# Layer 0 input stage: x before the adaLN loads, filter work mixed in by time, query latents stored to DRAM

## The chip, the cores and the metric

The kernel runs on one core of one Trainium2 chip. A core has five engines, each with its own instruction stream: TensorE (PE in the profile, with PEld for its weight loads), VectorE (DVE), ScalarE (ACT), GpSimd (POOL) and SyncE (SP). Here SP issues nearly all transfers and POOL a few; 16 DMA engines carry them. The metric is the time of one launch in microseconds on the device.

## The reference

A two-layer trunk over 1024 latent tokens and 256 context tokens of width 1024, in float32. Layer 0 is multi-head latent attention, layer 1 a Hyena long convolution. What matters here:

```python
shift, scale, gate = split((silu_c @ ada_w[i] + ada_b[i]), 3)       # adaLN, both layers
a  = modulate(rmsnorm(x, norm_g[0]), shift, scale)                  # latents
ac = modulate(rmsnorm(ctx, norm_g[0]), shift_c, scale_c)            # context
cq, ckv, k_rope, gate = split(t @ mla_w_in, splits)                 # t = a, then ac
q  = rmsnorm(cq, q_norm_g) @ w_uq;  kv = rmsnorm(ckv, kv_norm_g) @ w_ukv
...                                                                 # attention, output, residual
h = sin-MLP(features) @ hy_filt_w_out * decay                       # layer 1's filters
spec = rfft(k_circ(h))                                              # independent of x
```

## The kernel before

Tensors lie with channels on the 128 partitions. A matrix product is made of three float32r matmuls on high and low parts (`mm3`, L119 to L121): an operand is split by ScalarE (`hi`, L96) and VectorE (`lo`, L97). The program is written as Python generators that take turns. A scheduler then orders the instructions of each engine when the program is built, mostly in the order of writing, and fills in later ones where an engine would be free.

The stage in question is `layer0_in` (L440), about the first 440 us. It does three kinds of work side by side.

- **adaLN** (`ada`, L145): for k = 0 to 7 it loads a row block of the adaLN matrix and adds four packed matmuls (L128) to one PSUM bank `ad`; then it copies, transposes (L165) and adds the bias into `adac` and the gain `gs` (L171, L176). Layer 0's shift and scale take 32 pages of 128x512 (`pg<-in_adaw`). The rest (layer 1, and the gates) takes 32 tiles of 128x1024 (`aw`, two buffers).
- **Projections**: x is loaded in two halves of 512 tokens, normed (`rms`, L361; `spread`, L395) and modulated (`modulate`, L403) to `ax`, and `project` (L410) makes 14 column blocks: gates 0 to 7 (`gates`, stored to `gate_d`), the latents of key and value and the rotary key (`latent_kv`, stored to `ckv_d`, `kr_d`), and the query latents (`latent_q`). `context` does the same for the context tokens. Weights come through `wr` (two buffers) and are split to `w`.
- **Filters** (`filters`, L284): an MLP, then eight groups g. A group is eight steps j (load `dec`, four matmuls to `ph`, product `kk` at L321, sum and difference `kp`, `km`), a ring of vector sums (`ring`, L217), and eight blocks i, each split (`bh`, `bl`), multiplied with the matrices `fm` (`forward`, L267, PSUM `u`), scaled to `ko` and stored to `kd`. `rp`'s tiles have two buffers, `dec` too.

What sets the order: half 0 of x and its norm, then the 32 adaLN pages with a filter step after each k, and half 1 of x after k = 7. From then on one step of `work()` is taken for every two filter steps (`n * 120 < (step + 1) * 60`). When the filters are done their SBUF is given to the attention's tiles (`attention_loads`, L626): POOL loads `ckv`, `krh` and `krl`; the query latents come last and are split into SBUF tiles `cq` beside gates 6 and 7. SP is in order: a transfer that waits holds all behind it.

Of the kernel before, what the change touches and what calls it, by code (L numbers as in the profile page):

```python
# [11 lines left out]
F32 = mybir.dt.float32  # L12
# [43 lines left out]
class Net:  # L56
# [60 lines left out]
    def mm3(self, out, w, x, start, stop):  # L117
        mm = self.nc.tensor.matmul
        mm(out, lhsT=w[0], rhs=x[0], start=start, stop=False)  # L119
        mm(out, lhsT=w[0], rhs=x[1], start=False, stop=False)  # L120
        mm(out, lhsT=w[1], rhs=x[0], start=False, stop=stop)  # L121
# [23 lines left out]
    def ada(self, parts, page, bank, width):  # L145
# [138 lines left out]
    def filters(self, psum, pt_h, pt_u, side):  # L284
# [7 lines left out]
        for c in (slice(13, 19), slice(19, 25), slice(0, 7), slice(7, 13)):  # L292
            for i in range(2):
                nc.gpsimd.tensor_copy(out=fm[i][0:1, c.start, 0:1], in_=last[0:1, 0:1])
                nc.gpsimd.dma_start(out=fm[i][:, c], in_=a["fm"][i][:, c])
# [12 lines left out]
        for g in range(KD):  # L308
# [3 lines left out]
            for j in range(8):  # L312
                dec = rp.tile([P, 2, 1, P], F32, tag="dec", name="dec", bufs=2)
# [18 lines left out]
                yield  # L332
# [4 lines left out]
            def emit(i, b):  # L337
                u = self.forward(two, ubank, fm, i, b)
# [70 lines left out]

    def project(self, srcs, bank):  # L410
# [29 lines left out]
    def layer0_in(self):  # L440
# [12 lines left out]
        self.ckv_d = [self.dram.tile([KKV, P, NK], F32, name=f"ckv_d{r}") for r in range(2)]  # L453
        self.kr_d = [self.dram.tile([65, NK], F32, name=f"kr_d{r}") for r in range(2)]
        self.silu_c()
        self.feed([a["w1"][m] for m in (0, 1, 2, 8, 9, 10, 3, 4, 8, 9, 10, 5, 11, 12, 13, 6, 7)])
# [15 lines left out]
        load_x(0)  # L472
        rx = [self.rms(x[0], 512, bank, page)]
        filt.send(x[0][7])
        for n, _ in enumerate(self.ada([(0, 0, 4)], lambda n: page(), abank, 512)):
            next(filt)
            if n == 7:
                load_x(1)
# [937 lines left out]
```

## Time and profile before

| | us |
|---|---|
| median of 3 runs | 1739.24 (1736.87 to 1746.16) |
| the profiled execution | 1735.72 |
| its span, first to last instruction | 1733.9 |
| first projection matmul of layer 0 | 78.1 |
| last filter transform | 407.3 |
| first attention matmul on the stored latents | 436.6 |

A row of a table of groups reads: line, engine, operation, output<-inputs, shape, count, then busy time, mean ns of one, and idle time of the engine before it with what ended it. A row of the timeline reads: start, length, engine, line, operation, count, and in brackets the idle time before it and what ended that. In a table by stretch each engine has its busy time, with the number of instructions in brackets.

### The profile page before, as it was taken

Reading aid. Unit: us, or ns where it says so; the run is one execution under the profiler, and the core shown is the slowest. Engines: PE = TensorE matmul, PEld = TensorE weight load, DVE = VectorE, ACT = ScalarE, POOL = GpSimd, SP = SyncE. Lnnn points to the kernel's source line nnn. Section 1 sums busy time; section 2 is a strip of 40 time slices with the busy share of each in tenths; the row PEclk is TensorE's granted clock in tenths of the full one; section 3 lists DMA queues with packets and bytes.
Section 4 is the critical chain, followed back from the end, with each engine's and each line's share of the span. In section 5 each row is a group of like instructions: output and inputs, shape, how many; then the busy total and the mean of one; then the engine's idle time right before and its main releaser. Section 6 shows DMA issues by size and latency. Waiting matters only on the chain.

```text
span 1733.9 us, 22766 instructions
## 1 busy us (share of the span) xinstructions
PE 1635.3 (94%) x8096; PEld 1300.2 (75%) x8096; DVE 1442.4 (83%) x2539; ACT 766.1 (44%) x1331; POOL 15.4 (1%) x43
## 2 busy tenths in 40 slices
PE   6799897898999999999999999999999999999995
PEld 2467676686788788788787777888888888887873
DVE  4885978895598899899889466999999999999856
ACT  4533444435455555455556345433433433433313
POOL 1000000000000000000000010000000000000000
PEclk8899998999999999999999999999999999999998
DMA  9777563436101001010013781332332332334555
GB/s 341 255 231 222 182 191 118 147 95 196 37 22 42 25 26 37 25 33 25 19 56 121 233 268 64 101 97 84 100 117 83 104 111 85 102 113 138 175 158 204
DMA packets 139030, 207.19 MB, mean 119 GB/s; under 512 B 13386, under 2 KB 67361, under 8 KB 138788
## 3 DMA queue, kind: packets, MB, share of 16 engines
q1 hardware_dynamic: 135780, 195.05, 35.7%
q0 software_dynamic: 3136, 10.69, 1.9%
q8 instruction: 64, 1.05, 0.2%
q14 instruction: 50, 0.41, 0.1%
HBM read 149.97 MB, written 53.61 MB: 117 GB/s over the span
## 4 chain that ended last, share of the span: by engine, by line
PE 79%; DMA 8%; DVE 8%; ACT 3%; issue 1%; SPq 1%; DVEq 0%; ACTq 0%
PE pj L121 13%; PE pj L119 13%; PE pj L120 12%; PE O L120 2%; PE S L119 2%; PE O L119 2%; PE S L811 2%; DMA kd<-ko 2%; PE O L121 2%; PE apx L747 2%; PE S L810 2%; PE S L121 2%; PE S L120 2%; PE apx L748 2%; DMA aw<-in_adaw 2%; PE fu L119 2%
## 5 line engine op out<-in xcount | busy, mean ns | idle before, releaser
L96 ACT CAST w<-wr 128x512 fp32r<-128x512 f32 (+1 forms) x154 | 93.7, 609 | 259.2 <-PE pj L120 134.3
L119 PE MATMUL pj<-a,w 128*128 128x512 f32 x512 | 203.3, 398 | 1.7 <-ACT a L407 1.6
L121 PE MATMUL pj<-a,w 128*128 128x512 f32 x512 | 203.3, 398 | 0.0
L120 PE MATMUL pj<-a,w 128*128 128x512 f32 x512 | 203.2, 397 | 0.0
L813 ACT ACTIVATE p<-S 128x512 f32<-128x512 f32 x160 | 95.5, 597 | 148.2 <-DVE acc L820 69.5
L97 DVE TENSOR_TENSOR w<-wr,w 128x512 fp32r<-128x512 f32 (+1 forms) x154 | 102.4, 673 | 56.5 <-ACT w L96 56.3
L96 ACT CAST bh<-raw 128x512 fp32r<-128x512 f32 x128 | 77.0, 620 | 88.8 <-DVE raw L1056 71.1
L119 PEld LDWEIGHTS pj<-a,w 128*128 128x128 f32 x512 | 96.5, 189 | 22.0 <-ACT a L407 2.4
L120 PEld LDWEIGHTS pj<-a,w 128*128 128x128 f32 x512 | 96.6, 189 | 19.8 <-DVE a L408 0.2
L121 PEld LDWEIGHTS pj<-a,w 128*128 128x128 f32 x512 | 96.7, 189 | 19.4 <-issue 0.8
L97 DVE TENSOR_TENSOR p<-p 128x512 fp32r<-128x512 f32 x160 | 109.5, 685 | 1.5 <-ACT p L96 1.2
L749 DVE TENSOR_REDUCE cm<-apx 128x1 f32<-128x512 f32 (+1 forms) x192 | 107.3, 592 | 3.8 <-PE apx L748 3.0
L121 PE MATMUL pj<-pg,w 128*128 128x512 f32 (+1 forms) x248 | 98.0, 395 | 9.5 <-DVE w L97 9.5
L820 DVE TENSOR_TENSOR acc<-acc,p 128x512 f32<-128x512 f32 x144 | 98.9, 687 | 7.6 <-ACT p L813 6.7
L96 ACT CAST p<-p 128x512 fp32r<-128x512 f32 x160 | 99.4, 622 | 4.8
L119 PE MATMUL pj<-pg,w 128*128 128x512 f32 (+1 forms) x248 | 96.7, 393 | 2.4 <-ACT pg L407 2.4
L120 PE MATMUL pj<-pg,w 128*128 128x512 f32 (+1 forms) x248 | 98.1, 396 | 0.6 <-DVE pg L408 0.6
L97 DVE TENSOR_TENSOR bl<-raw,bh 128x512 fp32r<-128x512 f32 x128 | 84.9, 688 | 9.1 <-ACT bh L96 8.9
L119 PE MATMUL u<-bh,fm 128*128 128x256 f32 (+1 forms) x200 | 67.8, 340 | 11.6 <-ACT bh L96 9.0
L321 DVE TENSOR_TENSOR kk<-ph,dec 128x512 f32<-128x512 f32 x64 | 42.9, 685 | 35.4 <-DMA dec<-in_dec 28.2
L747 PE MATMUL apx<-kn,qn 128*128 128x512 f32 (+1 forms) x192 | 69.1, 364 | 2.3 <-DVE cm L749 1.9
L748 PE MATMUL apx<-krh,r 128*128 128x512 f32 (+1 forms) x192 | 67.2, 358 | 0.0
(304 smaller groups left out, 4392.4 us busy)
## 6 DMA issues: line engine op xcount, KB each, us to landing
aw<-in_adaw SPq DMA_DIRECT2D x32, 512.0 KB
kd<-ko SPq DMA_DIRECT2D x128, 128.0 KB
wr<-in_hw SPq DMA_DIRECT2D x64, 256.0 KB
kt<-kd SPq DMA_DIRECT2D x56, 256.0 KB
wr<-in_w SPq DMA_DIRECT2D x34, 256.0 KB
dec<-in_dec SPq DMA_DIRECT2D x64, 128.0 KB
pg<-in_adaw SPq DMA_DIRECT2D x32, 256.0 KB
wr<-in_wo SPq DMA_DIRECT2D x32, 256.0 KB
```

The costliest lines, as they stand in the source:

```text
L96: self.nc.scalar.copy(out=hi, in_=raw)
L97: self.nc.vector.tensor_tensor(out=lo, in0=raw, in1=hi, op=ALU.subtract)
L119: mm(out, lhsT=w[0], rhs=x[0], start=start, stop=False)
L120: mm(out, lhsT=w[0], rhs=x[1], start=False, stop=False)
L121: mm(out, lhsT=w[1], rhs=x[0], start=False, stop=stop)
L321: nc.vector.tensor_tensor(out=kk, in0=ps, in1=dec.broadcast_to([P, 2, 2, P]), op=ALU.mult)
L747: mm(b[:, :w], lhsT=qn[0][:, c], rhs=kn[0][:, o : o + w], start=True, stop=False)
L748: mm(b[:, :w], lhsT=r1[:, c], rhs=krh[:, o : o + w], start=False, stop=True)
L749: v.tensor_reduce(out=cm[:, t, i : i + 1], in_=b[:, :w], axis=AX.X, op=ALU.max)
L810: mm(S, lhsT=krh[:, c], rhs=r1, start=False, stop=False)
L813: act.activation(out=p, in_=S, func=AF.Exp, scale=ASCALE)
L820: v.tensor_tensor(out=acc, in0=acc, in1=p, op=ALU.add)
```

## The change

1. Both halves of x are loaded and multiplied by their inverse norm in place (`normalize`) before the adaLN loads. The modulate is then `shifted`: the high part by ScalarE with gain and shift, the same in place by VectorE (TENSOR_SCALAR), and the difference. Context does so inside `context`.
2. During layer 0's adaLN loads, the filters take a step only after every second k. The matrices `fm` are loaded in step j = 4 of group 0 rather than at the start, on POOL, behind a read of the last tile of x.
3. `ada` yields between its loads and its matmuls. For the later parts (`late`) the loads keep their written order, and the matmuls are placed behind the last matmul of a projection or filter (`self.last`). A step is taken at every third work step from the thirteenth on.
4. Filter steps yield a cost (1.5 for a step j, 9.0 to 1.5 for a block, ahead of it), and work steps are taken in proportion to the sum of costs: 61 over the stage. A filter block's matmuls are placed behind `self.last`.
5. `latent_q` runs in the middle, is stored to `cq_d` in DRAM as high and low parts, and POOL reloads it to `cq`. Gates 6 and 7 come after the attention loads.

PE runs the same 7928 matmuls, VectorE 2565 instructions in place of 2541, ScalarE 1331 in place of 1333 (two table loads fewer), POOL six more loads and SP twelve more stores.

```diff
-        self.feed([a["w1"][m] for m in (0, 1, 2, 8, 9, 10, 3, 4, 8, 9, 10, 5, 11, 12, 13, 6, 7)])
+        self.feed([a["w1"][m] for m in (0, 1, 8, 9, 10, 2, 3, 8, 9, 10, 11, 12, 13, 4, 5, 6, 7)])
...
-                    nc.sync.dma_start(out=w, in_=self.a["adaw"][layer, k, :, o : o + wd])
+                    dma = nc.sync.dma_start(out=w, in_=self.a["adaw"][layer, k, :, o : o + wd])
+                    if late:
+                        self.tc.keep_in_program_order(dma)
...
-            self.packed([(ps[32 * q : 32 * q + 32, :], self.sc[:, k, :], w, k == 0, k == KD - 1)
-                         for q, w in enumerate(cols)])
             yield
+            with self.tc.issue_after(self.last.ins) if late else ExitStack():
+                self.packed([(ps[32 * q : 32 * q + 32, :], self.sc[:, k, :], w, k == 0, k == KD - 1)
+                             for q, w in enumerate(cols)])
...
             for j in range(8):
+                if (g, j) == (0, 4):
+                    for c in (slice(13, 19), slice(19, 25), slice(0, 7), slice(7, 13)):
+                        for i in range(2):
+                            nc.gpsimd.tensor_copy(out=fm[i][0:1, c.start, 0:1], in_=last[0:1, 0:1])
+                            nc.gpsimd.dma_start(out=fm[i][:, c], in_=a["fm"][i][:, c])
...
-                yield
+                yield 1.5
...
-                u = self.forward(two, ubank, fm, i, b)
+                with self.tc.issue_after(self.last.ins):
+                    u = self.forward(two, ubank, fm, i, b)
...
+                yield {4: 9.0, 0: 2.1, 1: 2.1, 2: 2.8, 3: 2.1}.get(i, 1.5)
                 emit(i, b)
-                yield
...
+    def shifted(self, x, gs, sh, hi, lo):
+        nc = self.nc
+        nc.scalar.activation(out=hi, in_=x, func=AF.Identity, scale=gs, bias=sh)
+        nc.vector.tensor_scalar(out=x, in0=x, scalar1=gs, scalar2=sh, op0=ALU.mult, op1=ALU.add)
+        nc.vector.tensor_tensor(out=lo, in0=x, in1=hi, op=ALU.subtract)
...
+        for h, xs in enumerate(x):
+            load_x(h)
+            self.normalize(xs, self.rms(xs, 512, bank, page), bank)
+        begun = False
+        for n, _ in enumerate(self.ada([(0, 0, 4)], lambda n: page(), abank, 512, False)):
+            if n % 2:
+                if begun:
+                    next(filt)
+                else:
+                    filt.send(x[1][7])
+                    begun = True
...
+            yield from gates(range(0, 2))
             yield from latent_kv()
+            yield from gates(range(2, 4))
             yield from context()
+            yield from latent_q()
+            yield from gates(range(4, 6))
...
+        n, t, whole = 0, 0.0, 8 * (8 * 1.5 + 22.6) - 6.0
+        for cost in filt:
+            t += cost
+            while n * whole < t * 61:
                 next(todo, None)
                 n += 1
+                if n > 12 and n % 3 == 0:
+                    next(vecs, None)
...
+        for k in range(KQ):
+            for r in range(2):
+                nc.gpsimd.dma_start(out=cq[r][k], in_=self.cq_d[r][k])
```

How the change moves instructions is shown at three places. First SP's queue at the start of the program, where `in_xT` is x, `in_adaw` the adaLN matrix, `dec` the decay table of one filter step, `wr` a projection weight. Before, from the first half of x on:

```order
L466 DMA pg<-in_xT 128x512 x8
L303 DMA fwr<-in_fwout 128x512
L314 DMA dec<-in_dec 128x256
L324 DMA hbias<-in_hbias 1x2x128
L314 DMA dec<-in_dec 128x256
L112 DMA wr<-in_w 128x512 x2
L156 DMA aw<-in_adaw 128x1024 x2
L156 DMA pg<-in_adaw 128x512 x8
L314 DMA dec<-in_dec 128x256
L156 DMA pg<-in_adaw 128x512 x4
```

And in the changed kernel, from the same transfer on:

```order
L486 DMA pg<-in_xT 128x512 x8
L302 DMA fwr<-in_fwout 128x512
L318 DMA dec<-in_dec 128x256
L328 DMA hbias<-in_hbias 1x2x128
L318 DMA dec<-in_dec 128x256
L112 DMA wr<-in_w 128x512 x2
L486 DMA pg<-in_xT 128x512 x8
L318 DMA dec<-in_dec 128x256 x2
L302 DMA fwr<-in_fwout 128x512
L328 DMA hbias<-in_hbias 1x2x128
L156 DMA pg<-in_adaw 128x512 x32
L318 DMA dec<-in_dec 128x256 x2
```

The second half of x has moved ahead of the adaLN pages, which now stand in one piece behind two `dec` loads; the two early `aw` tiles are gone from there.

Second, VectorE where the adaLN result (`adac`, `gs`) arrives. In the changed kernel:

```order
L174 TENSOR_TENSOR adac_89<-ad,cols 128x4x4 x2
L179 SCALAR_TENSOR_TENSOR gs_90<-adac_89,cols 128x8
L332 TENSOR_TENSOR kp_342<-kk 128x256
L179 SCALAR_TENSOR_TENSOR gs_90<-adac_89,cols 128x8
L333 TENSOR_TENSOR km_344<-kk 128x256
L97 TENSOR_TENSOR fw<-fwr,fw 128x512
L97 TENSOR_TENSOR w<-wr,w 128x512
L426 TENSOR_SCALAR pg<-pg,gs_90,adac_89 128x512
L427 TENSOR_TENSOR pg<-pg 128x512
```

Before, at the same place:

```order
L171 TENSOR_TENSOR adac_87<-ad,cols 128x4x4
L176 SCALAR_TENSOR_TENSOR gs_88<-adac_87,cols 128x8
L321 TENSOR_TENSOR kk<-ph,dec 128x512
L388 RECIPROCAL rms<-rms 128x4
L176 SCALAR_TENSOR_TENSOR gs_88<-adac_87,cols 128x8
L328 TENSOR_TENSOR kp_954<-kk 128x256
L389 TENSOR_TENSOR rms<-rms 128x4
L97 TENSOR_TENSOR bl<-blk,bh 128x512
```

There filter group 0's blocks (`bl`) and the norm of the second half stand around it, and the modulate follows some fifteen instructions later; in the changed kernel the modulate follows at once and group 0's ring and blocks come between and after its tiles.

Third, POOL behind the filters. Before:

```order
L641 DMA ckv_3999<-ckv_d_81 128x1280
L641 DMA ckv_4000<-ckv_d_81 128x1280
L646 DMA krh<-kr_d_82 64x1280 x2
L647 DMA krl<-kr_d_83 65x1280
L969 CAST dm_9857<-x_9866 1x1
```

Changed:

```order
L657 DMA krh<-kr_d_84 64x1280 x2
L658 DMA krl<-kr_d_85 65x1280
L662 DMA cq_4332<-cq_d_82 128x1024
L662 DMA cq_4335<-cq_d_83 128x1024
L662 DMA cq_4333<-cq_d_82 128x1024
L662 DMA cq_4336<-cq_d_83 128x1024
L662 DMA cq_4334<-cq_d_82 128x1024
L662 DMA cq_4337<-cq_d_83 128x1024
```

The six reloads of the query latents stand last, behind the loads of the key and value latents.

More of the change, by code (lines that the diff above doesn't have):

```diff
@@ L120, in mm3 @@
         mm(out, lhsT=w[0], rhs=x[1], start=False, stop=False)
-        mm(out, lhsT=w[1], rhs=x[0], start=False, stop=stop)
+        self.last = mm(out, lhsT=w[1], rhs=x[0], start=False, stop=stop)
     def packed(self, mms):
@@ L143, in silu_c, with ada @@
                      for i in range(2)]
-    def ada(self, parts, page, bank, width):
+    def ada(self, parts, page, bank, width, late=True):
         nc = self.nc
@@ L291, in filters @@
         last = yield
[L292 to L295, printed above, removed]
         two = lambda tag, dt=F32: rp.tile([P, 2, CS], dt, tag=tag, name=tag)
@@ L408, in modulate, with normalize @@
         nc.vector.scalar_tensor_tensor(out=lo, in0=x, scalar=sh, in1=hi, op0=ALU.add, op1=ALU.subtract)
+    def normalize(self, xs, r, bank):
+        n = xs[0].shape[-1]
+        R = self.spread(r, n // P, bank)
+        for x in xs:
+            self.nc.vector.tensor_tensor(out=x, in0=x, in1=R[:, :n], op=ALU.mult)
+    def shifted(self, x, gs, sh, hi, lo):
[3 more added lines that the diff above has]
+        nc.vector.tensor_tensor(out=lo, in0=x, in1=hi, op=ALU.subtract)
     def project(self, srcs, bank):
@@ L453, in layer0_in @@
         self.ckv_d = [self.dram.tile([KKV, P, NK], F32, name=f"ckv_d{r}") for r in range(2)]
+        self.cq_d = [self.dram.tile([KQ, P, L], F32, name=f"cq_d{r}") for r in range(2)]
         self.kr_d = [self.dram.tile([65, NK], F32, name=f"kr_d{r}") for r in range(2)]
         self.silu_c()
-        self.feed([a["w1"][m] for m in (0, 1, 2, 8, 9, 10, 3, 4, 8, 9, 10, 5, 11, 12, 13, 6, 7)])
+        self.feed([a["w1"][m] for m in (0, 1, 8, 9, 10, 2, 3, 8, 9, 10, 11, 12, 13, 4, 5, 6, 7)])
         filt = self.filters(ps, "ph", "pu", "right")
@@ L509, in normed @@
             for k, t in enumerate(xs):
-                if sbuf:
-                    self.split(t, dst[0][k][:, sl], dst[1][k][:, sl])
-                else:
-                    hilo_out(t, P, [d[k, :, sl] for d in dst])
+                hilo_out(t, P, [d[k, :, sl] for d in dst])
         def context():
-            R = self.spread(rc, 2, bank)
+            self.normalize(xcs, self.rms(xcs, LC, bank, page), bank)
+            yield
             ac = [[], []]
@@ L571, in latent_q @@
                 yield
-            more = gates(range(6, 8))
             for h, sl in enumerate(halves):
-                for _ in normed([t[h] for t in ts], "qg", self.att[3], sl, True):
-                    next(more, None)
-                    yield
-            yield from more
+                yield from normed([t[h] for t in ts], "qg", self.cq_d, sl)
         def gates(ms):
@@ L588, in work @@
         def work():
[L589 to L592 removed]
+            yield from gates(range(0, 2))
             yield from latent_kv()
[L594 to L596 removed]
+            yield from gates(range(2, 4))
             yield from context()
[L598 to L607 removed]
+            yield from latent_q()
+            yield from gates(range(4, 6))
+        todo = work()
+        vecs = chain(self.ada([(1, 0, 4)], awt, abank, 1024), self.ada([(0, 4, 2), (1, 4, 2)], awt, abank, 1024))
+        n, t, whole = 0, 0.0, 8 * (8 * 1.5 + 22.6) - 6.0
+        for cost in filt:
+            t += cost
+            while n * whole < t * 61:
                 next(todo, None)
                 n += 1
+                if n > 12 and n % 3 == 0:
+                    next(vecs, None)
         for _ in todo:
+            pass
+        for _ in vecs:
             pass
@@ L618, in layer0_in @@
         next(loads)
-        for _ in latent_q():
-            next(loads, None)
         for _ in loads:
+            pass
+        for _ in gates(range(6, 8)):
             pass
```

37 lines of the change are left out of this document (5 added, 32 removed).

## The prediction

> **What bounds the kernel now.** I read the page's first two parts, then a table of busy time by stretch, then the timeline at the stretches' edges.
>
> ```profile
> span 1733.9 us, 22766 instructions
> PE 1635.3 (94%) x8096; PEld 1300.2 (75%) x8096; DVE 1442.4 (83%) x2539; ACT 766.1 (44%) x1331; POOL 15.4 (1%) x43
> PE   6799897898999999999999999999999999999995
> DVE  4885978895598899899889466999999999999856
> DMA  9777563436101001010013781332332332334555
> ```
>
> TensorE is 9 tenths busy nearly everywhere after slice 10 (a slice is 43.3 us). The gaps lie in the first ten slices, which are the layer 0 input stage, and that is the only place the change touches. Behind the first attention keys the built order of the two kernels is the same on every engine. The table below cuts that stage at the ends of the eight filter groups (the last split of a group, `bl`), from 107.5 us on; the two columns to compare are PE busy and DVE busy.
>
> ```profile
> core 0: us, PE busy (x) PEld busy (x) DVE busy (x) ACT busy (x) POOL busy (x), PEclk, DMA share, GB/s
> 0.00:61.00 61.00, 37.25 (x145) 14.01 (x145) 34.77 (x73) 24.00 (x39) 5.76 (x20) 0.80 0.98 339
> 61.00:78.00 17.00, 15.74 (x107) 11.21 (x108) 12.99 (x40) 11.25 (x27) 0.00 (x0) 0.90 0.67 191
> 78.00:107.50 29.50, 26.02 (x123) 16.12 (x122) 24.42 (x42) 17.10 (x27) 0.00 (x0) 0.94 0.59 187
> 107.50:142.00 34.50, 32.39 (x184) 23.81 (x187) 29.25 (x59) 13.39 (x24) 0.00 (x0) 1.00 0.81 254
> 142.00:194.00 52.00, 50.26 (x276) 39.55 (x268) 35.47 (x74) 18.59 (x34) 0.00 (x0) 0.97 0.58 175
> 194.00:240.00 46.00, 39.13 (x204) 31.18 (x203) 39.79 (x87) 19.59 (x35) 0.00 (x0) 0.93 0.65 200
> 240.00:289.00 49.00, 40.24 (x222) 32.70 (x221) 39.26 (x86) 21.03 (x39) 0.00 (x0) 0.94 0.53 164
> 289.00:331.00 42.00, 32.27 (x187) 27.70 (x186) 39.33 (x89) 17.32 (x34) 0.00 (x0) 0.87 0.47 137
> 331.00:371.00 40.00, 40.00 (x215) 33.76 (x214) 32.34 (x65) 16.86 (x29) 0.00 (x0) 1.00 0.38 114
> 371.00:407.00 36.00, 35.87 (x194) 29.61 (x193) 30.60 (x64) 18.92 (x34) 0.00 (x0) 1.00 0.41 119
> 407.00:441.00 34.00, 28.34 (x127) 21.40 (x125) 13.49 (x26) 13.38 (x24) 3.69 (x7) 0.95 0.74 215
> ```
>
> Three things are to be seen. Up to 61 us DMA is full (share 0.98) and both engines half idle. From 107.5 to 407 us VectorE is busy 246.0 of 299.5 us (82%) and PE 270.2 (90%): PE and DVE take turns as the bound, DVE at 289:331 (94%), PE at 331:371 (100%). From 407 us to the first attention work both wait for a reload.
>
> **Head: x, then the adaLN loads, then the tables.**
>
> ```profile
> 27.13 0.33 SPq L314 DMA_DIRECT2D dec<-in_dec  x1
> 52.34 1.94 PE L128 MATMUL ad<-pg,sc 128*32 128x512 f32 x8 [1.43 <-DMA pg<-in_adaw]
> 76.38 0.74 DVE L406 SCALAR_TENSOR_TENSOR pg<-pg,gs,pj 128x512 f32<-128x512 f32 x1
> 78.09 0.40 PE L119 MATMUL pj<-pg,w 128*128 128x512 f32 x1
> 28.00:54.00 26.00, 16.96 (x84) 6.00 (x80) 14.85 (x31) 1.05 (x2) 0.00 (x0) 0.70 1.05 373
> ```
>
> The adaLN product is complete at 54.3 us, yet the first modulate runs at 76.4 and the first projection at 78.1: the second half of x, its norm and filter group 0 stand between. In the changed order SP issues the third `dec` load before all 32 adaLN pages, and that load waits for the first kk product, as at 27.1 us now. So the pages start near 28.5 us; 32 x 256 KB are 8.4 MB, 22.5 us at the 373 GB/s of 28:54. They land near 53, with 1.5 us more for the landing. One product (1.94), the copy, transposes and sums (some 2 us, estimated) put the first modulate near 57 us: **19 us earlier**.
>
> That is not 19 us of gain, since what stood in between now comes later. In the built order VectorE has, from the adaLN result to the eighth `bl` of group 0, 49 instructions of 512 columns, 16 TENSOR_SCALAR, 26 of 256 and two of 1024.
>
> ```profile
> L321 DVE TENSOR_TENSOR kk<-ph,dec 128x512 f32<-128x512 f32 x64 | 42.9, 685 | 35.4 <-DMA dec<-in_dec 28.2 <-PE ph L319 6.7
> L328 DVE TENSOR_TENSOR kp<-kk 128x256 f32<-128x256 f32 x64 | 26.5, 417 | 0.5
> L225 DVE TENSOR_TENSOR rg<-kp,kp 128x1024 f32<-128x1024 f32 x16 | 18.8, 1220 | 0.0
> L408 DVE SCALAR_TENSOR_TENSOR pg<-pg,adac 128x512 fp32r<-128x512 f32 (+1 forms) x24 | 15.7, 656 | 3.9 <-ACT pg L407 3.9
> L406 DVE SCALAR_TENSOR_TENSOR pg<-pg,gs,pj 128x512 f32<-128x512 f32 (+1 forms) x24 | 15.2, 648 | 0.0
> L205 DVE TENSOR_SCALAR nrnd<-arg 128x512 f32<-128x512 f32 x6 | 2.6, 439 | 10.4 <-ACT arg L203 10.3
> DMA to landing us min/median/max: 7.7/11.6/15.7
> ```
>
> At 685, 439, 417 and 1220 ns that is 33.6 + 7.0 + 10.8 + 2.4 = 54 us. Back to back, rows overlap (two of 1220 ns in 2.35, two of 512 columns in 1.29), so 48 us is nearer: group 0 ends at 105 us if nothing waits. One new wait stands there: the filter matrices `fm` are now requested only when the last tile of x has been modulated, near 57 + 33 = 90 us, and the last row above gives their landing, 7.7 us at least. The third `bl` needs a product with them and stands some 42 us into this stretch, at 99, when the first piece lands. So between 0 and 12 us of wait (11.6 less nothing, the median landing with all of it bare); I take 5, since the DMA share is 0.6 there and not 1. Group 0 ends at **110 us against 107.3**: the head gives nothing by itself, but VectorE has then done the next group's first products too.
>
> **More work on VectorE.** Per tile the modulate was two instructions (L406 and L408, 648 and 656 ns on the mean of both widths); it becomes a normalise (no row; nearest L321, PSUM operand too, 685), a TENSOR_SCALAR (439) and a subtract (L97, 686). Bounds: +0 if the scalar form overlaps fully, +12 us if each of the 24 costs a whole 512-column step; from the rows +7 us. Sixteen normalises (11 us) fall into the load wait. Norm and split of the query latents, six of each at about 0.7 us, 8.4 us, ran after 407 us and now run before the filters end. What VectorE has from group 0's end to the filters' end was 246.0 us; the total to 407 was 318.2, grows by 7 + 8.4 to 333.6, and 82 are done by 110 us (72.2 before, and some 10 more counted from the order): **about 252 us**.
>
> **Filters mixed by time, adaLN pinned.** The eight groups keep their shape, some 21 us of products and ring, then eight transforms.
>
> ```profile
> 149.94 0.69 DVE L97 TENSOR_TENSOR w<-wr,w 128x512 fp32r<-128x512 f32 x1 [7.93 <-ACT w L96]
> 159.37 1.29 DVE L321 TENSOR_TENSOR kk<-ph,dec 128x512 f32<-128x512 f32 x2 [5.68 <-DMA dec<-in_dec]
> ACT w L96 <- DMA wr<-in_w: 21.8, 8, 9.4
> DVE kk L321 <- DMA dec<-in_dec: 17.3, 8, 5.7
> ```
>
> The two worst DVE gaps, 13.6 us in all in the stretch 142:194 (DVE 68%), come while SP steps through adaLN loads with `wr` and `dec` behind them. Pinning spreads the 16 later pairs over the whole stage, their matrix work three steps behind the load. If DVE were as busy in all seven groups as in the five without the adaLN knot (171.3 of 198.5 us, 86%), 252 us would take 292; at the 94% of 289:331 268; at today's 82% 307. I take 88%, 286 us: the two stretches at the end are 81 and 85% because PE works off its projections in lumps (PE 40.0 of 40), which an even mix shortens. The filters end at 110 + 286 = **396 us instead of 407.3**; bounds 378 and 417.
>
> **Tail: q spilled, gates last.**
>
> ```profile
> 407.80 0.53 POOL L641 DMA_DIRECT2D ckv<-ckv_d  x1 [389.73 <-PE u L121]
> 425.46 0.69 DVE L97 TENSOR_TENSOR cq<-pg,cq 128x512 fp32r<-128x512 f32 x1 [6.38 <-DMA kd<-ko]
> 429.93 0.79 PE L121 MATMUL pj<-pg,w 128*128 128x512 f32 x1 [4.76 <-DVE w L97]
> 436.62 0.39 PE L119 MATMUL pj<-ckv,wc 128*128 128x512 f32 x1
> 436.86 0.39 PE L120 MATMUL pj<-ckv,wc 128*128 128x512 f32 x1
> 440.91 0.50 PE L119 MATMUL pj<-cq,wb 128*128 128x512 f32 x1 [0.38 <-DVE kn L97]
> ```
>
> Now the last query split waits for the filter's stores until 425.5, a weight split is queued behind it on DVE, and PE stands 4.8 us; the first use of `cq` is 33.6 us after the last transform. In the changed order the split is gone from there; PE has some 85 projection matmuls (0.23 to 0.24 us from start to start) and the keys (436.6 to 440.9, 4.3), so it asks for `cq` 24 us after the last transform. Against that, POOL reloads 6 x 512 KB of `cq` behind `ckv`, `krh` and `krl` (3.6 MB): 6.75 MB, and SP's loads beside them some 2.8 MB. At the 373 GB/s above that is 26 us; at the 215 of 407:441 it is 44. I take 29, nearer the full rate since the queue is deep: gain 5 us, bounds +9 and -10.
>
> The Trainium skill, "DMA: Bandwidth & Descriptors", section "Issuing engines are not separate DMA queues", says that transfers of any issuing engine run on the same 16 DMA engines and interleave. By that the POOL reload hides behind nothing that SP moves; taken as free, the tail would gain 9, taken in series as above, 5. The row 407:441 (share 0.74 with POOL and SP both issuing) does not contradict it.
>
> **Sum.** The stage gives 11 (filters' end) and 5 (tail): 16 us. The profiled execution took 1735.7 us (span 1733.9 and 1.8 around it), so 1720; the median of the runs shown is 3.5 above it. I state **1721**.
>
> **Rivals.**
> *Nothing sticks.* DVE stays at its 82% because PE and DVE hold each other through two buffers, whatever the mix: filters end at 417, tail gains 5, net +5: 1741. For it: work between group ends, counted as the larger of PE's and DVE's, is about 268 us in both orders.
> *SP becomes the wait.* In the changed order the pinned adaLN loads stand ahead of `dec` and `wr` in every group, each waiting for its slot. If each of the eight groups meets the 5.7 us wait seen once, it is 46 us on DVE, less the 16: 1766; at half of it 1742. The point is whether the slot is free when SP arrives, that is whether PE has run the previous adaLN product; from five groups of eight on (28 us) it is slower than now. Against it: the product comes three steps after its load.
> *Reload in the way.* The loads run at the 215 GB/s of the row 407:441 and `cq` is there 44 us after the last transform, -10 in place of +5: 1735. This is what the skill's section above would lead to if the shared engines moved no more than they do now in that stretch.
> *It goes better.* DVE at 94% and no bare wait for `fm`: filters end at 373 to 378, 1696 to 1701.
>
> **Chances.** Forecast (1710 to 1730) 0.46; better 0.13; nothing sticks 0.19; SP 0.13; reload 0.09. The range 1696 to 1746 leaves out the worse half of the SP case and what lies beyond the ends of the others. What a measurement of this kernel can tell from no change is 0.5%, 8.7 us: faster 0.57 (the forecast nearly whole and the better case), same 0.28, slower 0.15 (most of the SP case, and two misses together).
>
> **What would show it.** First modulate near 57 us and first projection before 60; `fm` issued near 90 and the first transform by 100. Group 0 ended near 110. The DVE share in the seven groups, 88% or 82%, decides most; a `dec` or `wr` wait that grows beyond 17 and 22 us would show the SP rival, a wait for `cq` on PE the reload. If the head's 19 us stay as a gain, the count of what is put behind it was wrong.

## The result, and the profile after

The changed kernel takes 1769.35 us (median of 4, 1767.69 to 1771.82) against 1741.55 us for the kernel before on the same chip: a ratio of **1.017 (95% interval 1.015 to 1.019)**. It is slower by 1.7%; the forecast, 1721, was 1% faster. The profiled execution took 1768.48 us, its span is 1766.7. From the page:

```profile
span 1766.7 us, 22810 instructions
PE 1643.5 (93%) x8096; PEld 1304.2 (74%) x8096; DVE 1449.6 (82%) x2563; ACT 765.5 (43%) x1329; POOL 20.3 (1%) x49
PE   6788898979699999999999999999999999999996
DVE  6778697786289989899899746999999999999956
DMA  7473755556701111100002783232332233233545
```

The loss is all in the first eleven slices: the first product with `cq` starts at 476.0 us (440.9 before), and from there to the end it is 1290.7 us against 1293.0. The next table is that stage by stretch, cut at the first projection, at the point where VectorE runs dry, and at ends of filter groups (the last `bl` of each); three groups are left out. The columns are those of the table in the prediction.

```profile
0.00:63.00 63.00, 39.38 (x161) 15.69 (x161) 32.51 (x78) 26.30 (x45) 0.20 (x4) 0.81 0.78 268
63.00:103.00 40.00, 32.11 (x114) 23.23 (x114) 39.76 (x79) 17.50 (x26) 6.50 (x15) 0.79 0.20 59
103.00:121.00 18.00, 15.19 (x78) 13.39 (x79) 8.22 (x15) 6.27 (x11) 0.70 (x2) 0.81 1.10 362
...
150.50:204.00 53.50, 41.48 (x212) 31.06 (x211) 43.92 (x97) 21.06 (x38) 0.00 (x0) 0.81 0.55 170
204.00:248.00 44.00, 43.68 (x252) 33.77 (x250) 34.20 (x67) 19.57 (x36) 0.00 (x0) 1.00 0.68 209
...
340.00:389.00 49.00, 36.41 (x200) 27.38 (x199) 37.61 (x87) 18.10 (x34) 0.00 (x0) 0.86 0.60 188
389.00:431.00 42.00, 42.00 (x227) 32.91 (x225) 33.48 (x63) 17.23 (x30) 0.00 (x0) 1.00 0.70 226
431.00:476.00 45.00, 28.51 (x127) 22.06 (x125) 5.39 (x11) 8.96 (x18) 6.93 (x13) 0.81 0.87 264
```

VectorE (third number pair) is full at 63:103 and then has 8.2 of 18 us. In the middle the engines still take turns: PE 44 of 44 in one group, 41 of 53.5 in the one before. In the last row PE is idle for a third. The same view with two stretches, up to the end of group 0 and from there to the end of group 7, first before and then after:

```profile
0.00:107.30 107.30, 78.82 (x372) 41.24 (x372) 71.97 (x153) 52.35 (x91) 5.76 (x20) 0.86 0.82 274
107.30:406.10 298.80, 269.46 (x1464) 217.67 (x1462) 246.24 (x518) 125.69 (x228) 0.00 (x0) 0.95 0.55 166
```

```profile
0.00:120.80 120.80, 86.48 (x351) 52.16 (x352) 80.29 (x170) 50.07 (x81) 7.39 (x20) 0.80 0.63 212
120.80:430.90 310.10, 272.54 (x1488) 213.29 (x1488) 253.22 (x538) 131.17 (x243) 0.00 (x0) 0.92 0.58 179
```

The filters end 24.8 us later. VectorE has done 333.5 us of work by then instead of 318.2 (+15.3), and was idle for 97.4 instead of 87.9 (+9.5). The last transform starts at 432.5 us; from there to the first use of `cq` it is 43.5 us, 10 more than before. So there are three places: the head (+13.5 at group 0's end), groups 1 to 7 (+11.3, of which 7.0 are more work on VectorE), the tail (+10).

**Head.** The changed kernel's timeline of SP, PE, POOL and VectorE, and then two stretches of the table (its last numbers are granted clock, DMA share and GB/s):

```profile
28.66 1.00 SPq L318 DMA_DIRECT2D dec<-in_dec  x2
30.88 20.89 SPq L156 DMA_DIRECT2D pg<-in_adaw  x32
...
59.58 1.12 PE L168 MATMUL ad<-ident,pg 128*128 128x128 f32 x4
...
96.50 2.85 POOL L315 CAST fm<-pg 1x1 fp32r<-1x1 f32 x8 [96.06 <-DVE pg L426]
99.30 4.40 POOL L316 DMA_DIRECT2D fm<-in_fm  x8
...
110.20 0.69 DVE L97 TENSOR_TENSOR bl<-blk,bh 128x512 fp32r<-128x512 f32 x1 [7.02 <-ACT bh L96]
```

```profile
20.00:25.00 5.00, 1.72 (x12) 0.58 (x12) 3.42 (x8) 4.97 (x9) 0.00 (x0) 1.00 0.26 99
25.00:30.00 5.00, 3.75 (x14) 3.17 (x15) 4.42 (x11) 4.97 (x10) 0.00 (x0) 0.51 0.04 13
```

SP stands at the third `dec` until 28.7 us with the pages behind it, and DMA is nearly empty (share 0.26, then 0.04). The adaLN sums are transposed at 59.6 us. `fm` is asked for from 99 us on, behind a read of the last tile of x; VectorE runs dry at 103 and stands 7.0 us. The row names ScalarE's `bh`, the step before; that `fm` stands behind it is what e4_fm_at_adaln tests.

**Tail.** The changed kernel's timeline of SP and ScalarE, and its list of PE's waits at 430:480 (total, times, longest):

```profile
434.78 0.86 SPq L627 DMA_DIRECT2D aw<-in_watt  x1
...
436.87 10.66 SPq L356 DMA_DIRECT2D kd<-ko  x4
447.62 0.42 SPq L627 DMA_DIRECT2D aw<-in_watt  x1
...
445.95 0.60 ACT L345 ACTIVATE ko<-u 128x512 f32<-128x512 f32 x1 [9.10 <-DMA kd<-ko]
...
450.91 1.04 ACT L96 CAST wc<-aw 128x1024 fp32r<-128x1024 f32 x1 [3.86 <-DMA aw<-in_watt]
...
460.21 0.83 ACT L96 CAST wa<-aw 128x768 fp32r<-128x768 f32 x1 [7.84 <-DMA aw<-in_watt]
460.94 1.08 ACT L597 ACTIVATE st<-pj 128x512 f32<-128x512 f32 x2
```

```profile
PE pj L119 <- ACT st L597: 16.1, 1, 16.1
```

I read this as a chain. The last pinned adaLN pair holds both `aw` buffers until its product at 432.7 us, so the two raw attention weights (`in_watt`) that use them are asked for at 434.8 and 447.6, among and behind the last `kd` stores on SP. Those stores crawl beside POOL's reload. ScalarE stands at the weight splits (`wc` and `wa`, 3.9 and 7.8 us); the gates' Silu (`st`), which empties the projections' PSUM banks, comes behind them in its order; PE waits for it and stands 16.1 us. The experiments bear the chain out in part: where the weights come early the stand is gone, but e5_unit_costs and e7_old_head show that late weights alone do not make it.

### The profile page after: what moved, and what is told of

Read it like the earlier page. It is cut to its first block, busy times and chain, and to the rows that moved or that the text cites. A ratio compares the mean times of both kernels' runs of the same rounds, so it can differ in the third digit from the quotient of the medians.

```text
span 1766.7 us, 22810 instructions
## 1 busy us (share of the span) xinstructions
PE 1643.5 (93%) x8096; PEld 1304.2 (74%) x8096; DVE 1449.6 (82%) x2563; ACT 765.5 (43%) x1329; POOL 20.3 (1%) x49
## 3 DMA queue, kind: packets, MB, share of 16 engines
q8 instruction: 64, 1.05, 0.2%
## 4 chain that ended last, share of the span: by engine, by line
PE 70%; DVE 6%; DMA 5%; ACT 2%; issue 1%; SPq 1%; DVEq 0%; ACTq 0%
PE pj L121 11%; PE pj L119 11%; PE pj L120 11%; PE apx L761 2%; PE S L119 2%; PE apx L762 2%; PE O L120 2%; PE O L119 2%; PE S L825 2%; PE O L121 2%; PE S L824 2%; PE S L121 2%; PE S L120 2%; PE fu L119 2%; PE fy L119 2%; PE fy L121 2%
## 5 line engine op out<-in xcount | busy, mean ns | idle before, releaser
L827 ACT ACTIVATE p<-S 128x512 f32<-128x512 f32 x160 | 95.7, 598 | 147.6 <-DVE acc L834 71.9
L119 PE MATMUL pj<-pg,w 128*128 128x512 f32 (+1 forms) x248 | 100.3, 405 | 17.6 <-ACT st L597 16.1
L96 ACT CAST bh<-raw 128x512 fp32r<-128x512 f32 x128 | 77.1, 620 | 87.9 <-DVE raw L1070 70.9
L120 PE MATMUL pj<-pg,w 128*128 128x512 f32 (+1 forms) x248 | 99.0, 401 | 8.0 <-DVE pg L427 8.0
L121 PE MATMUL pj<-pg,w 128*128 128x512 f32 (+1 forms) x248 | 98.8, 400 | 4.4 <-DVE w L97 4.4
L119 PEld LDWEIGHTS pj<-pg,w 128*128 128x128 f32 x248 | 49.8, 201 | 32.2 <-ACT st L597 16.5
```

Source lines behind the costliest of these rows:

```text
L96: self.nc.scalar.copy(out=hi, in_=raw)
L121: self.last = mm(out, lhsT=w[1], rhs=x[0], start=False, stop=stop)
L827: act.activation(out=p, in_=S, func=AF.Exp, scale=ASCALE)
```

## The experiments

Ratios are to the kernel before on the same chip, with 95% intervals. "Last split" is the end of group 7.

### On the changed kernel

**e1_vecs_sooner**

```diff
-                if n > 12 and n % 3 == 0:
+                if n > 12 and n % 2 == 0:
```

> The changed kernel with one number altered: a step of the later adaLN work is taken at every second projection step instead of every third, so its last loads and products come well before the last filter group and the two 'aw' buffers are free for the raw attention weights early. Theory A (the raw attention weights are asked for only behind the last kd stores because their buffers are held, ACT stands in its queue for them, the gates' Silu and so the PSUM banks behind it): the 16.5 us in which PE waits for ACT at 445 to 461 us goes, the weights land before 430 us, first key product some 10 us sooner than 43 us after the last transform (about 33), span 1754 to 1759. Theory B (the reload of ckv, krh, krl and cq is the bound there): the same stretch ends within 3 us of where it does now, 1763 to 1767. Theory C (SP's loads ahead of dec cost the middle): with the loads denser the filter groups 1 to 5 end later by 3 us or more, and the gain in the tail is partly given back.

Ratio 1.0163 (1.0140 to 1.0185). The tail went from 43.5 to 26.8 us (A), with the weights asked for at 342 and 348 us, and PE's wait for the Silu is gone; the last split moved to 438.4, 7.5 us later (C). So the denser pinned loads give back nearly half, and in the times little is left: 1.0163 against 1.0172.

**e6_vecs_earlier**

```diff
-                if n > 12 and n % 3 == 0:
+                if n > 6 and n % 3 == 0:
```

> The changed kernel with the later adaLN work begun at projection step 9 instead of 15, at the same density (every third step), so it ends six steps sooner and the raw attention weights are asked for sooner, though still among the last kd stores. Theory A (held 'aw' buffers are what makes the tail 10 us longer, and density of the loads is what made the filter groups late in the denser run): filters end within 3 us of the changed kernel (430.9 for the last split), first cq product 27 to 36 us after the last transform instead of 43.5, span 1752 to 1762. Theory B (the reload of cq at shared DMA rate is the bound): 40 us or more after the last transform.

Ratio 1.0168 (1.0129 to 1.0207), no change in the times, though the tail is 26.7 us here too (cq at 464.3). The last split came at 436.1, 5 us later than in the changed kernel (3 at most was expected). ScalarE's rows at the same place, now without the wait for the weights:

```profile
443.83 0.59 ACT L597 ACTIVATE st<-pj 128x512 f32<-128x512 f32 x1
444.31 1.05 ACT L96 CAST wc<-aw 128x1024 fp32r<-128x1024 f32 x1
445.25 0.85 ACT L96 CAST wa<-aw 128x768 fp32r<-128x768 f32 x1
```

**e2_no_pin**

```diff
-                    if late:
-                        self.tc.keep_in_program_order(dma)
...
-            with self.tc.issue_after(self.last.ins) if late else ExitStack():
+            with ExitStack():
```

> The changed kernel with the pinning of the later adaLN work taken out: its loads may move up SP's order and its products stand where the scheduler puts them, as before the change. Theory 'SP becomes the wait' (pinned loads standing ahead of dec and wr): the DVE wait for dec in 100 to 420 us falls from 24.3 to 17 us or less and groups 1 to 7 take 303 us or less instead of 310.1. Theory 'the mix is it' (PE and DVE hold each other through two buffers): within 3 us of 310.1. Theory 'the pin helps': groups 1 to 7 take 313 or more, since unpinned loads knot in the first groups as they did before the change.

Ratio 1.0114 (1.0083 to 1.0146): 0.6% faster than the changed kernel. The waits of VectorE in groups 1 to 7, changed kernel first, then this one:

```profile
DVE kk L325 <- DMA dec<-in_dec: 24.3, 11, 5.3
```

```profile
DVE kk L323 <- DMA dec<-in_dec: 15.0, 14, 3.8
```

The wait for `dec` fell by 9 us, and groups 1 to 7 took 310.5 us, as they did with the pins (310.1). So in the changed kernel `dec` behind SP's queue is not what sets their length. The gain is the tail again: 26.5 us. PE's wait for adaLN tiles in the groups, too small for the list with the pins, is 10.9 us without them.

**e4_fm_at_adaln**

```diff
-     nc.gpsimd.tensor_copy(out=fm[i][0:1, c.start, 0:1], in_=last[0:1, 0:1])
+     nc.gpsimd.tensor_copy(out=fm[i][0:1, c.start, 0:1], in_=self.adac[0][1][0:1, 0, 0:1])
```

> The changed kernel with the filter matrices fm requested as soon as the adaLN result stands (about 60 us) instead of behind the last tile of x (96.3 us). Theory A (fm's landing is the whole of the 7.0 us stand of VectorE at 103 to 110 and what follows it): first transform at 84 to 92 us, group 0 ends at 110 to 113 instead of 120.8, and the 7 to 10 us carry through to the filters' end (421 to 424 instead of 430.9), span 1757 to 1760. Theory B (PE is full of projections there, so the transforms only change places with them): group 0 ends sooner, but group 2's end moves by less than 3 us and the span by less than 3 us.

Group 0 ended at 109.5 (A), 11.3 us sooner, so `fm` is what VectorE's stand waits for; the last split came at 425.7, 5.2 sooner, so half is left. The ratio is 1.0181 (1.0152 to 1.0211), no gain, and even the half is read from a lucky profile: the profiled execution, 1759.9, was the fastest of four (the others 1766.7 to 1769.4).

**h1_pages_in_hole**

```diff
-                    dma = nc.sync.dma_start(out=w, in_=...)
+                    if not late and k == 0:
+                        nc.gpsimd.tensor_copy(out=w[0:1, 0:1], in_=self.landed[0:1, 0:1])
+                    q = nc.sync if late else nc.gpsimd
+                    dma = q.dma_start(out=w, in_=...)
...
+        self.landed = x[1][7]
+        next(head)
```

> The changed kernel with fm requested at the adaLN result, and besides with the 32 adaLN pages of the head requested from POOL as soon as the last tile of x has landed (about 21 us), so that they don't stand behind SP's wait for the third dec slot (28.6 us). In the changed kernel the DMA share is 0.26 and 0.04 at 20 to 30 us. Theory A (that hole is what makes the adaLN result late): pages landed by 46 to 50 us instead of 58.8, first projection at 50 to 55 instead of 63, group 0 ends at 99 to 104 instead of 109.5, last split at 416 to 421. Theory B (VectorE's own work up to group 0's end, 78 us, sets it): first projection sooner, but group 0's end within 3 us of 109.5.

This edit stands on that of e4. A miss: ratio 1.0169 (1.0134 to 1.0203). The pages now began at 19.7 us and were all asked for by 49, but `dec` came late behind them (VectorE stood 5.3 us at 41), the normalises and group 0's ring were put ahead of the adaLN result on VectorE, and the first projection was at 70.9. Group 0 ended at 113.5, outside what both theories named. Since the edit moved `dec` and VectorE's order too, the run does not show what the empty stretch of DMA costs.

**e5_unit_costs**

```diff
-  whole = 8 * (8 * 1.5 + 22.6) - 6.0
+  whole = 124.0
...
-            t += cost
+            t += 1.0
```

> The changed kernel with the mixing by steps of equal cost (124 steps) instead of the times given with each yield. Theory A (the mixing by time puts projections where VectorE then waits): groups 1 to 7 take 300 to 305 us instead of 310.1. Theory B (the mix does not matter, the two engines hold each other either way): 307 to 313 us. Theory C (mixing by time is worth its while): 314 us or more.

Ratio 1.0152 (1.0126 to 1.0179), within the intervals of the changed kernel. Groups 1 to 7 took 317.2 us (C by the mark set, the last split 8 us later), and the tail, which no theory spoke of, 24.2. ScalarE in that tail:

```profile
442.04 0.61 ACT L597 ACTIVATE st<-pj 128x512 f32<-128x512 f32 x1
...
445.17 0.60 ACT L597 ACTIVATE st<-pj 128x512 f32<-128x512 f32 x1 [2.03 <-PE pj L121]
...
459.05 0.83 ACT L96 CAST wa<-aw 128x768 fp32r<-128x768 f32 x1 [8.77 <-DMA aw<-in_watt]
```

The weights were asked for behind the last transform here too, at 441.6 and 444.2 us, and ScalarE stood for them as long as in the changed kernel. But two Silus came ahead of the weight splits, and PE did not wait for a Silu. In the changed kernel, in e4 and in h1 none comes ahead of them, and these are the three tails of 42 to 43.5 us. On the other side stands f1, where the weights come early, all Silus come behind the splits, and PE does not wait for one either. So by these runs the stand needs both late weights and the Silus behind the splits. In e1, e2 and e6 a Silu also came ahead of the splits, so these changed both; no run alters the order of the Silus alone.

**e7_old_head**

```diff
-        for h, xs in enumerate(x):
-            load_x(h)
-            self.normalize(xs, self.rms(xs, 512, bank, page), bank)
+        load_x(0)
+        rx = [self.rms(x[0], 512, bank, page)]
+        filt.send(x[0][7])
...
-                if (g, j) == (0, 4):
+                if (g, j) == (0, 0):
...
-                self.shifted(xs[k], gs[:, k, 0:1], res[:, k, 0:1], hi, lo)
+                self.modulate(xs[k], R, gs[:, k, 0:1], res[:, k, 0:1], hi, lo)
```

> The changed kernel with the head of before (half of x, filter matrices at once, adaLN pages, group 0's products, the second half of x, modulate with the norm in it); the mix by time, the pins and the spill stay. Theory A (the new head is worth its loss of 13.5 us at group 0's end, all of it lasting): group 0 ends near 107, last split at 416 to 421, span 1752 to 1756. Theory B (what the head loses is made up, since projections that begin at 63 instead of 78 us leave TensorE less behind): group 0 near 107 but last split at 424 or later, span 1760 or more. The tail, with its buffers held, keeps its 43 us in both.

Ratio **1.0056** (1.0036 to 1.0077): two thirds of the loss is gone. Group 0 ended at 95.7, sooner than before the change (107.3); why is not shown, since f1, which only moves the later adaLN work out of it, ends at 105.6. The last split came at 414.8, 16 us sooner than in the changed kernel and a little sooner than A named. The tail took 32.4, where both theories said that it keeps its 43: the weights were late here too (asked for at 418.3 and 428.7, behind the last transform), but one Silu came ahead of their splits. The edit also alters the constant in the sum of costs (21 in place of 6).

### On the kernel before

**b10_spill_only**

```diff
             for _ in gen:
                 pass
+            yield from latent_q()
...
-        for _ in latent_q():
-            next(loads, None)
         for _ in loads:
             pass
+        for _ in gates(range(6, 8)):
+            pass
...
+        for k in range(KQ):
+            for r in range(2):
+                nc.gpsimd.dma_start(out=cq[r][k], in_=self.cq_d[r][k])
```

> The kernel before with the query projection among the filters, spilled, and the last two gates at the end; head, mix and adaLN order as before. The raw attention weights are still asked for well before the filters end. Theory A (the spill is a gain in the tail where the weights are early, and its 8.4 us of VectorE work and its projections move ahead of the filters' end): last transform at 413 to 418 instead of 407.3, cq used 24 to 29 us after it instead of 33.6, span 1733 to 1740. Theory B (the reload at the rate of the tail binds): cq used 36 us or more after the last transform, span 1744 or more. Theory C (projections in place of idle TensorE time): last transform within 3 us of 407.3, span 1730 or less.

Ratio 1.0060 (1.0040 to 1.0081). The last transform at 414.1 (A), but `cq` used 37.6 us after it (B, by a wait that neither theory named): here the query latents are normed just before the filters end, their stores hold the page slots, and ScalarE and then POOL wait for these.

```profile
433.65 0.62 ACT L96 CAST pg<-pg 128x512 fp32r<-128x512 f32 x1 [12.62 <-DMA cq_d<-pg]
...
436.81 2.28 POOL L649 DMA_DIRECT2D cq<-cq_d  x4 [18.38 <-DMA cq_d<-pg]
```

**b9_new_head_only**

```diff
-        load_x(0)
-        rx = [self.rms(x[0], 512, bank, page)]
-        filt.send(x[0][7])
+        for h, xs in enumerate(x):
+            load_x(h)
+            self.normalize(xs, self.rms(xs, 512, bank, page), bank)
...
-                self.modulate(xs[k], R, gs[:, k, 0:1], res[:, k, 0:1], hi, lo)
+                self.shifted(xs[k], gs[:, k, 0:1], res[:, k, 0:1], hi, lo)
```

> The kernel before with the new head alone (all of x, adaLN pages, then the tables; normalise, scale and subtract), fm requested as the adaLN result stands; no mix by time, no pin, query latents at the end as before. Theory A (with the fm wait gone the new head costs only its extra VectorE work): group 0 ends at 108 to 112, filters end at 408 to 414, tail 33 us, span 1736 to 1743. Theory B (work put behind the adaLN result, with TensorE's projections begun sooner, is a gain in groups 1 and 2, where VectorE was only 68% busy): filters end at 400 or sooner, span 1728 or less. Theory C (something else in the new order costs): filters end at 418 or later, span 1746 or more.

Ratio 1.0065 (1.0037 to 1.0092), the last split at 423.7 (C). Group 0 ended at 120.7 and group 1 took 56 us: the later adaLN loads stand in these groups. In g1, where they do not, group 1 took 40. So the run mixes two costs; f1 and g1 part them.

**f1_later_adaln**

```diff
-            for _ in gates(range(0, 3)):
-                next(gen, None)
-                yield
+            yield from gates(range(0, 3))
...
                 next(todo, None)
                 n += 1
+                if n > 6 and n % 2 == 0:
+                    next(vecs, None)
```

> The kernel before with one thing altered: the later adaLN work is not begun beside the first gates but from projection step 8 on, at every second step; nothing is pinned, head, mix and query latents are as before. Theory A (the later adaLN loads and products, standing between wr, dec and the first groups' products, are the 10 us of VectorE idle time that the changed kernel with the old head did not have): group 0 ends at 96 to 100 instead of 107.3 and groups 1 to 7 keep their 299 us, last split at 394 to 399, span 1720 to 1727. Theory B (TensorE's work is only put off, and the later groups are TensorE bound): last split at 403 or later, span 1731 or more.

Ratio **0.9933** (0.9909 to 0.9957), 1726.5 us: faster than both kernels. The last split came at 398.4 (A), but not by the way A named: group 0 ended at 105.6, and the gain is in group 2. There PE was the bound; first before, then here:

```profile
141.70:193.90 52.20, 50.45 (x275) 39.51 (x276) 35.67 (x75) 18.59 (x34) 0.00 (x0) 0.97 0.58 175
```

```profile
140.20:176.50 36.30, 36.30 (x201) 29.00 (x199) 29.93 (x59) 14.16 (x26) 0.00 (x0) 1.00 0.55 171
```

PE has 14 us less work in it, and groups 3 and 4 take back 10. Of the 12.9 us by which `cq` is used sooner, 7.7 are at the last split and 5.3 in the tail (28.3 us against 33.6), which no theory named.

**f2_later_pinned**, against f1

```diff
+                    if late:
+                        self.tc.keep_in_program_order(dma)
...
             yield
+            with self.tc.issue_after(self.last.ins) if late else ExitStack():
+                self.packed([...
```

> As the run before, with the pins of the change besides (the loads keep the program's order on SP, the products stand behind the last one emitted). Theory 'SP becomes the wait': groups 1 to 7 take 5 us or more longer than unpinned, and VectorE's wait for dec in the filter stage is above 25 us. Theory 'the pin is harmless': within 3 us of the unpinned run. Beside the changed kernel with the old head (last split 414.8, groups 1 to 7 319 us) it lacks the mix by time and the spill: if those are what costs there, the last split is at 400 or sooner.

Ratio 1.0032 (1.0014 to 1.0049): the pins cost 1.0%. Groups 1 to 7 took 307.7 us against 292.8. VectorE's wait for `dec` was 7.2 us, less than in f1, so the named sign of "SP becomes the wait" is absent; PE itself waited 13.3 us for adaLN tiles (1.5 in f1), and VectorE's busy share fell from 84 to 80%. The tail took 33.6 us, 5 more than in f1. VectorE and PE in the list of waits of f2, from the end of group 0 to the end of group 7:

```profile
PE ad L128 <- DMA aw<-in_adaw: 13.3, 8, 3.2
DVE kk L324 <- DMA dec<-in_dec: 7.2, 6, 2.2
```

**m1_timed_mix**, against f1

```diff
-                yield
+                yield 1.5
...
+                yield {4: 9.0, 0: 2.1, 1: 2.1, 2: 2.8, 3: 2.1}.get(i, 1.5)
                 emit(i, b)
-                yield
...
-            while n * 120 < (step + 1) * 60:
+            while n * whole < t * 60:
```

> The run with the later adaLN work moved to step 8 on (unpinned, 0.9933 of before), and in it only the mix by time: the yields carry their times, a yield stands ahead of each transform, and projections are taken by the share of that time that has gone by, 60 steps over the whole as before. Theory A (an even mix shortens the stretches in which one engine waits, the step of the prediction with 88%): groups 1 to 7 take 285 us or less instead of 292.8, VectorE busy 84% or more in them, span 1715 or less. Theory B (the two engines hold each other through two buffers, whatever the mix): 290 to 296 us, span within 3 us of 1724.6. Theory C (mixing by time costs): 298 us or more, span 1729 or more.

Ratio 0.9936 (0.9916 to 0.9956): the mix by time is worth nothing (B; groups 1 to 7 took 296.7 us, 0.7 above its mark, 292.8 in f1). The last split came at 398.6 (398.4 in f1), VectorE was 83% busy in groups 1 to 7 (84% in f1). The edit leaves out the other half of the change's fourth point, the transforms placed behind `self.last`.

**g1_head_on_f1**: f1 with the edit of b9_new_head_only.

> The run f1 (0.9933 of before, group 0 ended at 105.6, last split 398.4) with the new head and fm requested at the adaLN result. It differs from f1 in the head alone and has neither pin, spill nor mix by time. Theory A (the head costs by itself, by its extra VectorE work and the waits for pages, some 14 us at group 0's end of which most lasts): last split 404 to 412, ratio 0.997 to 1.002. Theory B (in a stage without the pins the earlier projections make the head's loss good): last split within 3 us of 398.4, ratio 0.991 to 0.995.

Ratio 1.0020 (0.9999 to 1.0041), 0.9% above f1 (A). The first projection came 12 us sooner (67.7), group 0 ended 11 later (116.7), the last split at 405.8, the tail took 33.5 us against 28.3. Of the 11 us at group 0's end only 2.4 are more work on VectorE (74.8 us against 72.4); the rest is idle time. In groups 1 to 7 it was 86% busy (247.2 of 289.1 us).

**g2_head_fm_late**, against g1

```diff
-     nc.gpsimd.tensor_copy(out=fm[i][0:1, c.start, 0:1], in_=self.adac[0][1][0:1, 0, 0:1])
+     nc.gpsimd.tensor_copy(out=fm[i][0:1, c.start, 0:1], in_=last[0:1, 0:1])
```

> As the run before, but fm requested behind the last tile of x, as in the change. Theory A (VectorE stands some 7 us for fm's landing and the loss lasts): group 0 ends 8 to 12 us later than in the run before, last split 5 us or more later, ratio higher by 0.003 or more. Theory B (the lost time is made up, since TensorE's work is only shifted): group 0 later, but ratio within 0.002.

Ratio 1.0044 (1.0023 to 1.0065). Group 0 ended at 132.6, 16 later than in g1, the last split at 411.6, 5.8 later. Group 1 was 7 us shorter, and the tail 5.6. In time it is 0.24%, between the marks of A and B and inside the two intervals.

**g3_no_pin_fm**: the changed kernel with the edits of e2_no_pin and e4_fm_at_adaln.

> The changed kernel without the pins (1.0114 of before) and with fm requested at the adaLN result. If the wait for fm costs time of its own, the ratio is 1.003 to 1.008; if what it costs at group 0's end is lost again in the middle, as the times of the run with fm alone say (1.0181 against 1.0172 for the changed kernel), it stays at 1.010 to 1.013.

Ratio 1.0094 (1.0068 to 1.0119), between the two ranges named and 0.2% below e2_no_pin: if it is a gain, it is a small one, inside the intervals.

### The account

| part | runs compared | difference of ratios |
|---|---|---|
| later adaLN work moved out of the first groups | f1 to before | -0.7% |
| mix by time | m1 to f1 | 0.0% |
| pins | f2 to f1 | +1.0% |
| new head, `fm` early | g1 to f1 | +0.9% |
| `fm` late | g2 to g1 | +0.2% |
| spill, gates last | b10 to before | +0.6% |

Together +2.0%, some 35 us, against +1.7% measured. Each difference is uncertain by some 0.3%, and the parts were taken alone, on two different kernels, in a stage where one wait hides another, so the agreement is weak evidence that nothing large is missing, no more. Two things stand in no row: the transforms placed behind `self.last`, which no run takes out alone, and the change's own start of the later adaLN work (from step 13, every third) in place of f1's (from step 8, every second). In the changed kernel itself the head is worth 1.2% (e7) and the pins 0.6% (e2).

## Why the prediction was wrong

`cq` was forecast for about 425 us and came at 476.0. Of the 50 us, 11 had arisen by group 0's end, 24 in groups 1 to 7 and 15 in the tail.

**First modulate near 57, first projection before 60.** Measured 63 for both. The third `dec` was issued at 28.66 (28.5 forecast), but the pages started at 30.9 into an empty DMA queue. The adaLN sums were transposed from 59.6 on, some four us late, and from there to VectorE's first modulate (63.4) it was four more, where the forecast had about two from the last product. The 1.5 us of landing in that sum is a term that no run shows by itself.

**"I take 5" for the wait for `fm`; group 0 ends at 110.** It ended at 120.8. Six us came with the late start (63 for 57). From there VectorE had 48.0 us of work, as forecast, and stood 10 rather than 5: 7.0 us at once before the third `bl`, most of the rest right behind it. The mechanism was right, the term mis-sized by five us. Its price in time is less: half is left at the last split (e4), and 0.2% in the times, inside the intervals (g2, g3).

**VectorE's work, 333.6 us to the filters' end.** Measured 333.5. This term was right, and 252 us for groups 1 to 7 (253.2) too.

**"I take 88%, 286 us."** This is the step that failed most. VectorE was busy 253.2 of 310.1 us, 82% as before; 24 of the 35 us by which group 7 ended later than forecast. The prediction took the uneven mix to be what keeps the share low. m1 shows that the even mix leaves the groups as they are, and e5 that taking it out does not gain. No run reached 88%: VectorE's share in these groups lies between 80 and 86%, lowest in pinned runs (80% in f2 and e5) and highest with the new head on f1 (g1 and g2, 86%), where group 0 is longer for it. The rival "nothing sticks" was right on the share, and its reason, that PE and DVE hold each other through two buffers, agrees with the rows: in either order one of them is full in one group and idle in the next, and the larger of the two busy times, summed over the groups, is 278 us before and 281 after (268 in both by the prediction's count). That the buffers are what does it is argued; no run alters their number, and none takes out the transforms' place behind `self.last`. What sets the 82% in the changed kernel stays open.

**Tail: 24 us and 5 for the reload.** Measured 43.5. The step took the arrival of the attention weights as given, and ScalarE's Silu with it. The `aw` buffers, held by the pinned work, move the weights behind the last stores, and the Silus stand behind the weights' splits. Where the buffers were free in time (e1, e2, e6) `cq` was used 26.5 to 26.8 us after the last transform, and where the Silus came first (e5) 24.2: the forecast 29 is near, and "reload in the way" falls.

**"SP becomes the wait"** gave a time near the measured one (1766), but not for its reason. Its sign, a longer wait for `dec`, was there (24.3 us against 17.3), and taking it away left the groups as long (e2). In the changed kernel the pins' price shows in the tail (e2). On f1 it is the groups that grow, by 15 us, and PE's 13.3 us of waiting for adaLN tiles grow with them (f2); in the changed kernel that wait is not there. The forecast named neither.

**The head as a whole** was put at no gain. e7 and g1 show that it costs 0.9 to 1.2%. The sum counted its extra VectorE work; in g1 most of the 11 us at group 0's end is idle time on VectorE. In e7 the tail changed as well, so the 1.2% is not the head's alone.

**The stated time.** The prediction's own terms, 1720 and 3.5 for the median, give 1723 or 1724; 1721 was stated. Beside an error of 48 us this does not matter.

## What to carry to other kernels

When loads are pinned to a late place, ask who needs their buffers next, and follow the queues to the end: here two buffers held too long made a weight load late, and with the Silus queued behind that weight's split TensorE stood for 16 us. Count each engine's work by stretch before moving it: f1 gained by taking 14 us of TensorE's work out of a group in which TensorE was full. Do not raise a busy share in a sum unless a run has shown it. Of the five edits made together one half of one, taken alone and begun earlier (f1), was worth having, so time them one by one.

## What the runs showed of the hardware

A store of 128 KB to `kd` that took its place beside POOL's reload was waited for 9.1 us by ScalarE, and the chain of waits gives it 11.65 us, while the 16 engines were full (a stretch of the changed kernel, and a piece of its chain):

```profile
432.00:446.00 14.00, 13.53 (x68) 10.19 (x66) 0.39 (x4) 1.24 (x3) 6.06 (x12) 1.00 1.05 308
```

```profile
434.23 11.65 DMA kd<-ko
```

The Trainium skill, "DMA: Bandwidth & Descriptors", section "Issuing engines are not separate DMA queues", says that transfers of different issuing engines interleave on the same 16 DMA engines; the trace agrees, with a share of 1.05 while SP's stores and POOL's loads were under way together.

The profiled execution is one draw. e4 and e6 ran from 1759 to 1769 and 1772 us, and in both the profile was of the fastest. Behind the first use of `cq` before and after have one order, and no experiment edits that part, yet it took 1289 to 1302 us. What makes it vary stays open; an end of a stage read from one profile is good to a few us, not better.
